# Two gate units moved from between the steps of grouped-query attention into the block-pair stage of a hybrid encoder block

## The chip, the core and the metric

The kernel runs as one program on one core of a Trainium2 chip. The metric is the device time of one execution in microseconds (us), as the median of several runs. Five engines work side by side, each through its own queue of instructions in a fixed order: TensorE (PE, matrix products; its weight loads are listed as PEld), VectorE (DVE), ScalarE (ACT), GpSimd (POOL) and SyncE (SP, which issues most transfers). An instruction starts when those ahead of it on its engine have started or ended and its semaphores are there.

## The reference

One encoder layer over 1024 tokens of width 1024 with three parallel mixers. Cut to what matters here:

```python
h = rms_norm(x, g_pre)
a_qkv, bq, bk, bv, mq, ga, gb, gm, mg = split(h @ w_in)   # one wide projection
oa = dilated window attention of a_qkv (3 groups, softmax-weighted over the groups)
ob = grouped-query attention: 8 query heads, 2 key heads, all 1024 tokens
om = cross-attention into 256 memory rows
ya = (oa * silu(ga)) @ w_br_a
yb = (ob * silu(gb)) @ w_br_b
ym = (om * silu(gm)) @ w_br_m
gates = sigmoid(mg + b_merge)
merged = gates[0] * ya + gates[1] * yb + gates[2] * ym
out = x + rms_norm(merged @ w_out, g_post)
```

The change concerns `ga`, 512 of the columns of `h @ w_in`. They are four *gate units* of 128 columns, named (0, 0) to (0, 3). `gb` is the units (1, 0) to (1, 3), `gm` the units (2, 0) to (2, 3). Each unit ends as g * (1 + tanh(g / 2)), which is twice the silu, and is stored in DRAM (`g2d`).

## The kernel before

Products of h are made in a split form: h and each weight are a high part and a rest (`hh` and `hl`, `wh` and `wl`), and a product of 128 rows by 512 tokens is three matmuls: high by high, high by rest, rest by high.

**A gate unit multiplied plainly** (`add_unit`, L187, and `dense`, L125) loads 512 KB of weights, splits them (ACT L91, DVE L92), and makes for each of two halves of the tokens 8 x 3 = 24 matmuls with a moving tile of 512 columns (PE L129, L131, L133): 48 for a unit, 96 for two. Each half is finished by `evac` in `add_gate` (L198): DVE L200, ACT L201, DVE L202 and a store (L203).

**The attention stage** (`b_att`, L770) is grouped-query attention as 16 groups (8 blocks of 128 queries by 2 key heads), 8 steps to a group. Step n does `row_max` on PE (L781, its minimum taken by DVE L782), and for later stages of earlier steps: `shift` (PE transpose L789, DVE L790), `scores` (PE L799 and L800, exponential on ACT L802, running sum on POOL: L804 for the second key tile of a group, L806 for the third to the eighth), `pv` once in 8 steps (8 matmuls of L815, each listed as two, on plain 32-bit data), and `final` one step behind it: the sum is split (ACT L91 into `blh`, DVE L92 into `bll`) and summed over partitions by two PE matmuls (L111). `q_prep` (four PE transposes L704, ACT L707, DVE L709, ACT L711) comes once in 16 steps.

PE's order is written by hand. `weave` (L162) takes matmuls one at a time from two sources, the queue of gate units and the attention, so that both come to an end together: it compares the share done of each by a table of costs, and so spreads the gate matmuls evenly between the attention's steps. The attention's estimate holds pads (`START_PAD`, `END_PAD`) where it has nothing for PE. Before the change seven units are spread over the attention: (2, 3), (1, 0) to (1, 3), (0, 0) and (0, 1). The other engines' order in this stage comes from a scheduler.

**The pair stage** (from L1326, its products in `pair_product`, L1314) multiplies units two at a time in a Winograd form of Strassen's method: 2 x 2 blocks, seven products in place of eight, each 4 x 3 = 12 matmuls of 512 columns, so 84 for a pair of units. The sums of weight blocks that it needs are POOL's (`k_sum`, L1067), the splits ACT's and DVE's (`k_block`, `k_own`), the sums of results DVE's (`c_add`, `c_fin`). The list `PAIRS` gives the order: 12 pairs of rotary units alternate with the others, which are one pair of gate units, (0, 2) and (0, 3), and 12 pairs of merge units, 25 pairs in all. The weights of pair n are loaded two pairs ahead (`k_load`), in turn into the `wr` buffers and into two tiles named `vA12`. In this stage all engines' orders are written by hand.

Between the two stages lie the products of the values (L1233 and L1284); behind the pairs come the windowed attention, the branch projections and the output.

Of the kernel before, what the change touches and what calls it, by code (L numbers as in the profile page):

```python
# [8 lines left out]
F32 = mybir.dt.float32  # L9
# [8 lines left out]
P = 128  # L18
# [15 lines left out]
def block(ctx: ExitStack, tc: tile.TileContext, x, xT, memT, cst, msk, bcst, tabA, gpost,  # L34
          wu, wv, wb, wmem, wbr, wout, out):
    nc = tc.nc
# [160 lines left out]
    def add_gate(i, p_):  # L197
        def evac(half, p):  # L198
            th = fp["p"].tile([P, 512], F32, name="fth", bufs=2)
            V.tensor_tensor(th, p, rb[:, half * 512:half * 512 + 512], op=OP.mult)  # L200
            A.activation(p, th, AF.Tanh, scale=0.5)  # L201
            V.scalar_tensor_tensor(th, p, 1.0, th, op0=OP.add, op1=OP.mult)  # L202
            nc.sync.dma_start(g2d[i, p_, :, half * 512:half * 512 + 512], th)  # L203
        add_unit(wu[U_G + 4 * i + p_], evac)

    g2d = dram.tile([3, 4, P, S], F32, name="g2d")
# [12 lines left out]
    def pool(name, side="left"):  # L219
        p = tc.tile_pool(name=name, bufs=1, side=side, reuse_waits="tile")  # L220
        return p, p.__enter__()
# [226 lines left out]
    for k in range(8):  # L448
        if k % 2 == 0:
            load_wkv(k // 2)  # L450
        for e in range(2 if k == 0 else 1):
            t = slice(e * 512, e * 512 + 512) if k == 0 else slice(0, S)
# [29 lines left out]
    for c in range(2):  # L482
        t = st.tile([P, 4, 256], F32, name=f"mt{c}", tag=f"xk{c}")
# [209 lines left out]
    half = [slice(0, 512), slice(512, 1024)]  # L693
    with tc.tile_pool(name="ba", bufs=1, reuse_waits="tile") as ba:
# [185 lines left out]
        ng = 0  # L880
        for i in (2, 1, 0):
            for p_ in range(4):
                if (i, p_) not in ((2, 0), (2, 1), (2, 2)) + GATES_P:
                    add_gate(i, p_)
                    ng += 1
        early[len(queue)] = first_values
# [23 lines left out]
    vbp, vb = pool("vb", "right")  # L910
# [128 lines left out]

    TURNS = [(j, c, g) for c in range(2) for g in range(3) for j in (1, 0)]  # L1040
    pairs = [(8 * i + f, 8 * i + f + 1) for i in (2, 1, 0) for f in range(0, 8, 2)]
    others = [("gate", 0)] + [("merge", m) for m in range(12)]
    PAIRS = [x for m in range(12) for x in (("rope", m), others[m])] + [others[12]]
    KR = {}

    def unit_of(n, u):
        kind, m = PAIRS[n]
        if kind == "rope":
            return 2 * m + u
        return U_M + pairs[m][u] if kind == "merge" else U_G + 4 * GATES_P[u][0] + GATES_P[u][1]  # L1050

    def k_load(n, u):

        KR[n, u] = (vb.tile([P, 1024], F32, name=f"vA12{u}") if n % 2 else
                    wp.tile([P, 1024], F32, name="wr", bufs=WR))
        nc.sync.dma_start(KR[n, u], wu[unit_of(n, u)])

# [46 lines left out]
    def kr():  # L1104
        z = next(kr_turn) % 10
        return (vb.tile([P, 512], F32, name=("vy2", "vy3", "vv0", "vv1", "vy0", "vy1")[z]) if z < 6 else
                SPARE[z // 2 - 3][:, half[z % 2]])
# [7 lines left out]
    def c_fin(n, u, t, ps_=None):  # L1115

        r = RV.pop((n, u, t)) if ps_ is None else kr() if n < last else p1
        src = r if ps_ is None else ps_
        kind, m = PAIRS[n]
        if kind != "rope":  # L1120
            V.tensor_tensor(r, src, rb[:, half[t]], op=OP.mult)
            if kind == "gate":
                x = kr()

                def gate_it():
                    A.activation(x, r, AF.Tanh, scale=0.5)
                    V.scalar_tensor_tensor(r, x, 1.0, r, op0=OP.add, op1=OP.mult)
                    nc.sync.dma_start(g2d[GATES_P[u]][:, half[t]], r)
                then.append(gate_it)
            else:  # L1130
                j = pairs[m][u]

                def merge_it():
                    A.activation(r, r, AF.Tanh, scale=0.5, bias=hbm[:, j:j + 1])
                    nc.scalar.dma_start(thd[j, :, half[t]], r)
                then.append(merge_it)
            return
        x = kr()
        if TURNS[m][0]:
            V.tensor_tensor(x, src, tab[0][:, half[t]], op=OP.mult)  # L1140
            V.tensor_tensor(r, src, tab[1][:, half[t]], op=OP.mult)
        else:
            V.scalar_tensor_tensor(x, src, -0.125, tab[0][:, half[t]], op0=OP.mult, op1=OP.mult)
            V.scalar_tensor_tensor(r, src, -0.125, tab[1][:, half[t]], op0=OP.mult, op1=OP.mult)
        RP[m, t, u] = x, r

    def turn_it(n, t):
        kind, m = PAIRS[n]
        if kind != "rope":
            return  # L1150
        g = TURNS[m][2]
        (ac, as_), (bc, bs) = [RP.pop((m, t, z)) for z in range(2)]
        if m not in RO:
            RO[m] = [kp.tile([P, S], F32, name=f"ko{z}") for z in range(2)]
        o1, o2 = RO[m]
        G.tensor_tensor(half_of(o1, t, g), classes(ac, g), classes(bs, g), op=OP.subtract)
        G.tensor_tensor(half_of(o2, t, g), classes(as_, g), classes(bc, g), op=OP.add)

    def k_store(n):
        kind, m = PAIRS[n]  # L1160
        if kind != "rope":
            return
        j, c, g = TURNS[m]
        for u, o in enumerate(RO.pop(m)):
            for h in range(4):
                a = h % 2 * 64 + 32 * u
                nc.sync.dma_start(qkd[j, 2 * c + h // 2, g, a:a + 32], o[h * 32:h * 32 + 32])
# [57 lines left out]
    for n in range(28):  # L1225
        i, k = divmod(n, 4)
# [17 lines left out]
        for stage in (2, 1, 0):  # L1244
            r, at = divmod(n - 6 - (0, 2, 3)[stage], 3)
# [14 lines left out]
        if k == 3:  # L1260
# [4 lines left out]
            7: [lambda: operand(7, 1), lambda: operand(7, 2)], 8: [lambda: v3_split("S3")],  # L1265
            9: [lambda: [nc.sync.dma_start(tab[j], tabA[:, j]) for j in range(2)]],
            13: [lambda: k_load(0, 0), lambda: V.tensor_tensor(tab[1], tab[1], rb, op=OP.mult)],
            17: [lambda: V.tensor_tensor(tab[0], tab[0], rb, op=OP.mult)],
            10: [lambda: v3_sum("S4", "A12", "S2", OP.subtract)], 12: [lambda: v3_split("S4")],
            14: [lambda: v3_sum("S1", "A11", "S2", OP.add)], 16: [lambda: v3_split("S1")],  # L1270
            18: [lambda: k_load(0, 1)], 20: [lambda: v3_split("A22"), lambda: k_load(1, 0)], 22: [lambda: k_load(1, 1)],
            23: [lambda: k_sum(0, 1)], 24: [lambda: k_own(0)], 25: [lambda: [k_sum(0, j) for j in (2, 3)]],
            26: [lambda: k_block(0, "S2")], 27: [lambda: k_block(0, "S1"), lambda: k_block(0, "S3"), lambda: k_sum(0, 4)]}
    for n in range(28):
        i, k = divmod(n, 4)
# [33 lines left out]
    SPARE = [wp.tile([P, 1024], F32, name=x) for x in ("wh", "wl")]  # L1309
    last = len(PAIRS) - 1  # L1310
    BANK = {}
# [90 lines left out]
    for n in range(last + 1):  # L1402
# [31 lines left out]
        if n + 2 <= last:  # L1434
            k_load(n + 2, 0)
# [41 lines left out]
    r = RV[last, 0, 1]  # L1477
# [741 lines left out]
    q, r = ss[7], ss[7][:, 3:4]  # L2219
# [33 lines left out]
ATT_PRIO = 120  # L2253
LA_T, LA_P = 2, 3
FIRST_PAD, LAST_PAD = 7000.0, 2000.0
GATES_P = ((0, 2), (0, 3))
VG = (2, 0, 1)
U_G = 24
U_MQ = 36
U_M = 40  # L2260
# [112 lines left out]
```

## Time and profile before

| What | us |
|---|---|
| median of 3 runs (1364.65 to 1366.45) | 1366.28 |
| the profiled execution, device time | 1364.44 |
| its span, first to last instruction | 1362.5 |
| attention stage, from the first `row_max` on PE to the first matmul of the values | 212.8 to 453.2 |
| pair stage, its 2100 matmuls | 569.86 to 1046.22 |
| PE busy over the span | 1344.7 |

A line of the timeline has the start in us, the duration, the engine, the line of the code, the operation, output and inputs with their shapes, the count that was merged, and in brackets how long the engine was idle ahead of it and what ended that. In a table of windows each engine has its busy time in the stretch and the number of its instructions. Matmuls overlap, so the step from one to the next is read from two starts, not from a duration.

### The profile page before, as it was taken

What the parts mean: (1) busy time and instruction counts of PE and PEld (TensorE: products, weight loads), DVE (VectorE), ACT (ScalarE), POOL (GpSimd) and SP (SyncE); (2) the same over time, 40 slices, a digit from 0 to 9 for tenths busy, and PEclk for the clock granted to TensorE, in tenths of its full rate; (3) what the DMA queues carried; (4) which work ended last, traced back from release to release, by engine and by line L of the source; (5) the groups of instructions that cost most, each with busy time, mean ns of one, the idle gap of its engine ahead of it and who ended that gap; (6) DMA issues with size and microseconds to landing.
All of it is one profiled execution on the core that took longest, in us unless ns stands there. A gap on an engine that the chain in (4) does not pass through costs nothing.

```text
span 1362.5 us, 22863 instructions
## 1 busy us (share of the span) xinstructions
PE 1344.7 (99%) x8303; PEld 1087.4 (80%) x8303; DVE 1016.6 (75%) x1837; ACT 657.1 (48%) x1389; POOL 579.1 (43%) x443
## 2 busy tenths in 40 slices
PE   7999999999999999999999999999999999999997
PEld 7899986666666789988888888888888777778886
DVE  7868677776777498767777776687877666778977
ACT  7544465656655445333343333333335676763332
POOL 0516702676676200244465554555552135662003
PEclk9999999999999999999999999999999999999999
DMA  6346522322244578514333333322347777976445
GB/s 253 109 170 232 179 108 94 104 78 93 74 132 142 210 239 277 164 57 138 99 114 118 108 124 123 115 91 91 107 129 256 233 209 244 279 231 233 146 187 185
DMA packets 125488, 213.80 MB, mean 157 GB/s; under 512 B 32480, under 2 KB 64576, under 8 KB 125376
## 3 DMA queue, kind: packets, MB, share of 16 engines
q1 hardware_dynamic: 116064, 198.42, 44.7%
q10 hardware_dynamic: 9312, 13.93, 2.8%
q8 instruction: 65, 1.06, 0.3%
q14 instruction: 47, 0.39, 0.1%
HBM read 145.92 MB, written 66.38 MB: 156 GB/s over the span
## 4 chain that ended last, share of the span: by engine, by line
PE 93%; DVE 3%; ACT 2%; issue 1%; POOL 1%; DMA 0%; SPq 0%; DVEq 0%; POOLq 0%; ACTq 0%
PE s L1323 35%; PE d L1913 7%; PE s L1233 4%; PE s L2137 4%; PE ov L815 4%; PE sc L2055 3%; PE d L133 3%; PE d L129 3%; PE d L131 3%; PE s L1284 3%; PE s L1597 2%; PE tr L781 2%; PE s L800 2%; PE s L799 2%; PE d L529 2%; PE d L2137 2%
## 5 line engine op out<-in xcount | busy, mean ns | idle before, releaser
L806 POOL TENSOR_TENSOR bl<-bl,bp 128x512 f32<-128x512 f32 x96 | 132.9, 1384 | 52.8 <-ACT bp L802 47.3
L1323 PE MATMUL s<-hh,vS 128*128 128x512 f32 x400 | 131.1, 389 | 0.0
L1323 PE MATMUL s<-vA,vS 128*128 128x512 f32 x450 | 106.1, 389 | 0.0
L92 DVE TENSOR_TENSOR vS<-vot,vS 128x512 fp32r<-128x512 f32 x75 | 89.4, 1193 | 19.9 <-ACT vS L91 19.9
L1323 PEld LDWEIGHTS s<-vA,vS 128*128 128x128 f32 x450 | 84.5, 188 | 17.5
L802 ACT ACTIVATE bp<-s 128x512 f32<-128x512 f32 x128 | 75.7, 595 | 43.2 <-PE s L800 42.2
L782 DVE TENSOR_REDUCE bn<-tr 128x1 f32<-128x512 f32 x128 | 85.2, 683 | 12.5 <-PE tr L781 11.5
L133 PE MATMUL d<-hh,wl 128*128 128x512 f32 x224 | 89.5, 400 | 0.0
L131 PE MATMUL d<-hl,wh 128*128 128x512 f32 x224 | 89.1, 398 | 0.0
L129 PE MATMUL d<-hh,wh 128*128 128x512 f32 x224 | 89.0, 397 | 0.0
L1323 PEld LDWEIGHTS s<-hh,vS 128*128 128x128 f32 x400 | 75.1, 188 | 15.6
L1609 ACT ACTIVATE pra<-pra,sts 128x192 f32<-128x192 f32 (+1 forms) x176 | 72.4, 415 | 13.3 <-DVE sts L1608 13.1
L1323 PE MATMUL s<-hh,wl 128*128 128x512 f32 x200 | 78.1, 390 | 0.0
L1323 PE MATMUL s<-hl,wh 128*128 128x512 f32 x200 | 77.8, 389 | 0.0
L1323 PE MATMUL s<-hh,wh 128*128 128x512 f32 x200 | 77.8, 389 | 0.0
L1323 PE MATMUL s<-hl,vS 128*128 128x512 f32 x200 | 77.8, 389 | 0.0
L1608 DVE CUSTOM_DVE_ANT_0 pra<-s,mask 128x192 f32<-128x192 f32 (+1 forms) x192 | 48.8, 309 | 33.5 <-PE s L1597 20.0
L1327 ACT ACTIVATE vv<-s 128x512 f32<-128x512 f32 x50 | 29.9, 598 | 82.3 <-PE s L1323 48.4
L1067 POOL TENSOR_TENSOR vot<-wr 128x512 f32<-128x512 f32 x13 | 22.2, 1706 | 111.0 <-DVE wl L92 111.0
L815 PE MATMUL ov<-bp,VS 128*64 128x512 f32 x256 | 58.5, 598 | 0.0
L1067 POOL TENSOR_TENSOR vot<-vot,vA 128x512 f32<-128x512 f32 x12 | 19.3, 1606 | 89.7 <-DVE vS L92 89.7
L129 PEld LDWEIGHTS d<-hh,wh 128*128 128x128 f32 x224 | 42.2, 188 | 13.3 <-issue 5.3
(627 smaller groups left out, 4004.6 us busy)
## 6 DMA issues: line engine op xcount, KB each, us to landing
wr<-in_wu SPq DMA_DIRECT2D x40, 512.0 KB
vA<-in_wu SPq DMA_DIRECT2D x24, 512.0 KB
qkd<-ko SPq DMA_DIRECT2D x96, 128.0 KB
wl<-thd SPq DMA_DIRECT2D x24, 512.0 KB
wos<-os SPq DMA_DIRECT2D x12, 512.0 KB
wr<-in_wbr SPq DMA_DIRECT2D x24, 256.0 KB
aq<-qkd SPq DMA_DIRECT2D x12, 512.0 KB
ak<-qkd SPq DMA_DIRECT2D x12, 512.0 KB
```

The costliest lines, as they stand in the source:

```text
L92: V.tensor_tensor(dst_l, src, dst_h.bitcast(F32), op=OP.subtract)
L129: PE.matmul(dst, wh[:, k, :], hh[k][:, t], start=k == 0, stop=False)
L131: PE.matmul(dst, wh[:, k, :], hl[k][:, t], start=False, stop=False)
L133: PE.matmul(dst, wl[:, k, :], hh[k][:, t], start=False, stop=k == 7)
L782: fp["last"] = V.tensor_reduce(st[i]["n"][:, j, c:c + 1], s, axis=AX.X, op=OP.min)
L802: A.activation(pp, s, AF.Exp, scale=-1.0)
L806: G.tensor_tensor(lsum[i % 2], lsum[i % 2], pp, op=OP.add)
L815: PE.matmul(o[e * 64:e * 64 + 64], VS[:, kt, kv], d.pop(kt), start=kt < 2, stop=kt >= NT - 2)
L1323: PE.matmul(BANK[n, c], a, b, start=k == 0 and q == 0 and not more, stop=k == 3 and q == 2, skip_group_check=c in "XW")
L1609: A.activation(src, src, AF.Exp, scale=-1.0, bias=bias, accum_out=sts[:, 1, h, T:T + 1])
L1913: PE.matmul(ps_, a, b, start=k == 0 and q == 0, stop=k == 3 and q == 2)
L2137: PE.matmul(dst[:, e[0]:e[1]], a, b, start=k == 0 and q == 0, stop=k == 3 and q == 2)
```

## The change

The two units (0, 0) and (0, 1) leave the queue of the attention stage, which keeps five. They become a second gate pair, `("gate", 0)`, of the pair stage; the old gate pair becomes `("gate", 1)`. There are 26 pairs: gate pairs stand second and fourth, each merge pair comes one place later among the others, and the list ends in three merge pairs in place of two. So that the last pair still has its weights in `wr`, the turn of the two buffers is counted from the end: the first pair now loads into `vA12`.

```diff
-                if (i, p_) not in ((2, 0), (2, 1), (2, 2)) + GATES_P:
+                if (i, p_) not in ((2, 0), (2, 1), (2, 2)) + sum(GATES_P, ()):
...
-    others = [("gate", 0)] + [("merge", m) for m in range(12)]
-    PAIRS = [x for m in range(12) for x in (("rope", m), others[m])] + [others[12]]
+    others = [("gate", m) for m in range(len(GATES_P))] + [("merge", m) for m in range(12)]
+    PAIRS = [x for m in range(12) for x in (("rope", m), others[m])] + others[12:]
...
-        return U_M + pairs[m][u] if kind == "merge" else U_G + 4 * GATES_P[u][0] + GATES_P[u][1]
+        if kind == "merge":
+            return U_M + pairs[m][u]
+        i, p_ = GATES_P[m][u]
+        return U_G + 4 * i + p_
...
-        KR[n, u] = (vb.tile([P, 1024], F32, name=f"vA12{u}") if n % 2 else
+        KR[n, u] = (vb.tile([P, 1024], F32, name=f"vA12{u}") if (len(PAIRS) - n) % 2 == 0 else
...
-                    nc.sync.dma_start(g2d[GATES_P[u]][:, half[t]], r)
+                    nc.sync.dma_start(g2d[GATES_P[m][u]][:, half[t]], r)
...
-GATES_P = ((0, 2), (0, 3))
+GATES_P = ((0, 0), (0, 1)), ((0, 2), (0, 3))
```

With five units in place of seven `weave` lays the gate matmuls thinner. Three places show it.

The first is PE's order in the middle of the attention, from the `pv` of the eighth group on (L129, L131 and L133 are gate matmuls, L781 a `row_max`, L799 and L800 the scores of one key tile, L111 the two sums of `final`). Before:

```order
L815 MATMUL ov<-bp,VS 64x512 x8
L133 MATMUL d<-hh_88,wl 128x512
L129 MATMUL d<-hh_89,wh 128x512
L131 MATMUL d<-hl_97,wh 128x512
L133 MATMUL d<-hh_89,wl 128x512
L129 MATMUL d<-hh_90,wh 128x512
L131 MATMUL d<-hl_98,wh 128x512
L133 MATMUL d<-hh_90,wl 128x512
L781 MATMUL tr<-KS,QH 128x512
L129 MATMUL d<-hh_91,wh 128x512
L799 MATMUL s_3945<-QH,KS 128x512
L800 MATMUL s_3945<-QL,KB 128x512
```

And of the change:

```order
L815 MATMUL ov<-bp,VS 64x512 x8
L133 MATMUL d<-hh_87,wl 128x512
L129 MATMUL d<-hh_88,wh 128x512
L131 MATMUL d<-hl_96,wh 128x512
L133 MATMUL d<-hh_88,wl 128x512
L129 MATMUL d<-hh_89,wh 128x512
L781 MATMUL tr<-KS,QH 128x512
L799 MATMUL s_3873<-QH,KS 128x512
L800 MATMUL s_3873<-QL,KB 128x512
```

Five gate matmuls follow a `pv` where there were seven, and none stands between the `row_max` and the scores. From one `pv` to the next of the 13 middle periods there are now 13 gate matmuls in each; before there were 17 to 19, 236 in all.

The second is PE's order at the stage's beginning, from the first `q_prep` (L704) on. Before:

```order
L704 MATMUL tr<-cs,qn_1025 128x128 x4
L131 MATMUL d<-hl_93,wh 128x512
L133 MATMUL d<-hh_85,wl 128x512
L129 MATMUL d<-hh_86,wh 128x512
L131 MATMUL d<-hl_94,wh 128x512
L133 MATMUL d<-hh_86,wl 128x512
L129 MATMUL d<-hh_87,wh 128x512
L131 MATMUL d<-hl_95,wh 128x512
L133 MATMUL d<-hh_87,wl 128x512
L129 MATMUL d<-hh_88,wh 128x512
L131 MATMUL d<-hl_96,wh 128x512
L781 MATMUL tr<-KS,QH 128x512
```

And of the change:

```order
L704 MATMUL tr<-cs,qn_1025 128x128 x4
L131 MATMUL d<-hl_93,wh 128x512
L133 MATMUL d<-hh_85,wl 128x512
L129 MATMUL d<-hh_86,wh 128x512
L131 MATMUL d<-hl_94,wh 128x512
L133 MATMUL d<-hh_86,wl 128x512
L129 MATMUL d<-hh_87,wh 128x512
L131 MATMUL d<-hl_95,wh 128x512
L781 MATMUL tr<-KS,QH 128x512
```

Seven gate matmuls lie between `q_prep` and the first `row_max` where there were ten. From there to the first `pv` there are 29 in place of 41. DVE has one L200 and no L202 in that stretch where it had two L200 and one L202.

The third is ACT's order at the stage's end, from the split of the sum of the last group but one (`blh`) on; the L802 behind it is the exponential of the last group's second key tile, L201 belongs to a gate unit, and the next L802 is the third key tile. Before:

```order
L91 ACTIVATE blh<-bl_2700 128x512
L802 ACTIVATE bp<-s_4864 128x512
L817 ACTIVATE obt<-ov 64x512
L201 ACTIVATE d<-fth 128x512
L802 ACTIVATE bp<-s_4898 128x512
```

And of the change:

```order
L91 ACTIVATE blh<-bl_2700 128x512
L802 ACTIVATE bp<-s_4747 128x512
L201 ACTIVATE d<-fth 128x512
L817 ACTIVATE obt<-ov 64x512
L802 ACTIVATE bp<-s_4772 128x512
```

The gate's L201 now stands ahead of L817, and still ahead of the third key tile's exponential. On PE there are 17 gate matmuls between that key tile's scores and the last `final` before the change and 13 behind it. From the `pv` that ends the middle (421.65 us) to the first matmul of the values there are 48 and 34.

## The prediction

> **What bounds the kernel now.** The page's first part comes first: one engine is busy nearly all the time.
>
> ```profile
> PE 1344.7 (99%) x8303; PEld 1087.4 (80%) x8303; DVE 1016.6 (75%) x1837; ACT 657.1 (48%) x1389; POOL 579.1 (43%) x443
> ```
>
> So a matmul fewer is time saved wherever PE stays the engine that others wait for, and the question is what is late next where matmuls go. The chain that ended last, in order of time, gives the two stages:
>
> ```profile
> 234.65 3.58 PE ov L815 x16
> ...
> 421.65 3.58 PE ov L815 x16
> ...
> 569.86 476.36 PE s L1323 x2100
> ```
>
> The last row is the whole pair stage: 2100 matmuls without a break, 476.36 / 2100 = 0.2268 us each. Nothing but PE is on the path there. The other two are the first and the fourteenth `pv`; 13 periods of the attention lie between them, 187.0 / 13 = 14.38 us each. The table of windows cuts the attention into middle, beginning and end:
>
> ```profile
> 234.65:421.65 187.00, 187.00 (x822) 120.73 (x823) 137.39 (x213) 113.55 (x186) 125.94 (x92) 1.00 0.32 104
> 212.80:234.65 21.85, 21.33 (x91) 15.61 (x93) 21.02 (x35) 13.88 (x20) 6.92 (x6) 1.00 0.28 97
> 421.65:453.30 31.65, 31.36 (x135) 18.12 (x135) 16.79 (x21) 16.61 (x30) 20.53 (x16) 1.00 0.20 68
> ```
>
> The columns behind the stretch are its length, then PE, PEld, DVE, ACT and POOL, then clock and DMA. The granted clock is full. In the middle PE has no idle time, DVE 73%, POOL 67%, ACT 61%. In the beginning DVE is busy 21.02 of 21.85 us, as full as PE: here two engines bind together.
>
> **Part 1, what goes.** 96 matmuls leave the attention. Their price is the step between gate matmuls that follow each other:
>
> ```profile
> 425.51 0.40 PE L131 MATMUL d<-hl,wh 128*128 128x512 f32 x1
> 425.75 0.40 PE L133 MATMUL d<-hh,wl 128*128 128x512 f32 x1
> 425.98 0.40 PE L129 MATMUL d<-hh,wh 128*128 128x512 f32 x1
> 426.22 0.40 PE L131 MATMUL d<-hl,wh 128*128 128x512 f32 x1
> 426.45 0.39 PE L133 MATMUL d<-hh,wl 128*128 128x512 f32 x1
> ```
>
> 0.94 us for four steps, 0.235 each: **-22.6 us** if PE stays the bound throughout. At the pair stage's pace it is -21.8, the other end.
>
> **Part 2, what comes.** One pair is 84 matmuls at 0.2268: **+19.05 us**. Its sums, splits and evacuations hide under PE as those of the 25 pairs do: over the pair stage DVE, the fullest helper, is busy 358.81 of 476.36 us.
>
> ```profile
> 569.86:1046.22 476.36, 476.36 (x2101) 393.90 (x2101) 358.81 (x383) 179.12 (x281) 244.37 (x146) 1.00 0.36 118
> ```
>
> A gate pair behind a rotary pair stands at the list's head already, between two rotary pairs and without a break, so the second one meets nothing new. The new turn of buffers puts the first pair into tiles whose last reader, the split of the fifth product of the values, is over before that stage ends; I cost it at nothing. What the loads have as cover is two pairs, 38 us, and without it the pair would wait for 512 KB at a time.
>
> Without any new wait the sum is -22.6 + 19.05 = -3.5 us (-2.7 at one pace for both). The Trainium skill, "TensorE: Matmul & The Clock Gate" (section "Wait — 56ns, not 53.3ns?"), gives one price for a warm matmul of 512 columns, 215.7 ns, wherever it stands. By it the change saves at most 12 x 0.2157 = 2.6 us, an estimate from that page; this trace has two paces, 0.227 and 0.235, both slower, and I go by them.
>
> **Part 3, what is late next.** The 96 matmuls are also cover: 15 of them at the beginning, 67 in the middle, 14 at the end (counted in the order). I take the three apart.
>
> *Beginning.* From `q_prep` to the first `row_max` runs a fixed chain through ACT:
>
> ```profile
> 209.71 0.60 PE L704 MATMUL tr<-cs,qn 128*128 128x128 f32 x4
> ...
> 212.79 0.50 PE L781 MATMUL tr<-KS,QH 128*128 128x512 f32 x1 [0.16 <-ACT QH L711]
> ...
> 220.28 0.50 PE L781 MATMUL tr<-KS,QH 128*128 128x512 f32 x1 [0.34 <-DVE bn L782]
> ```
>
> The chain is 3.08 us and PE waited for its end already, so the three matmuls that go there (0.7 us) save nothing. Behind it `row_max` waits for DVE to free a bank (third row). 12 matmuls go, 2.8 us; DVE loses one L200 and one L202, at 0.69 and 0.68:
>
> ```profile
> L202 DVE SCALAR_TENSOR_TENSOR fth<-d,fth 128x512 f32<-128x512 f32 x10 | 6.8, 683 | 0.7 <-ACT d L201 0.7
> L200 DVE TENSOR_TENSOR fth<-d,rb 128x512 f32<-128x512 f32 x9 | 6.2, 686 | 2.3 <-PE d L133 2.2
> ```
>
> Were DVE the bound all along, 1.4 of the 2.8 us would be lost; in the stretch's second half DVE has short waits for PE, so I take 0.5. Lost at the beginning: 0.7 + 0.5 = **1.2** (ends: 0 and the whole 3.5).
>
> *Middle.* 67 matmuls in 13 periods are 5.15 each, 1.21 us, so the period falls to 14.38 - 1.21 = 13.17. DVE had 137.39 / 13 = 10.6 us of work in it, POOL 9.7, ACT 8.7, and gate work goes from DVE and ACT; none reaches 13.17. What can bind is a loop. POOL's is the tightest: the sum's last addition, ACT's `blh`, the next group's exponential, L804, six L806.
>
> ```profile
> 266.46 1.31 POOL L804 TENSOR_TENSOR bl<-bp 128x512 f32<-128x512 f32 x1 [1.22 <-ACT bp L802]
> 270.63 8.92 POOL L806 TENSOR_TENSOR bl<-bl,bp 128x512 f32<-128x512 f32 x6 [2.87 <-ACT bp L802]
> 282.49 1.29 POOL L804 TENSOR_TENSOR bl<-bp 128x512 f32<-128x512 f32 x1 [2.94 <-ACT bp L802]
> ```
>
> Without the 2.87 us of waiting for PE's third key tile the loop is 8.92 + 2.94 + 1.29 = 13.15 us where ACT's four copies of `q_prep` stand in it (last row), and 1.22 + 1.31 + 8.92 = 11.45 where they don't (first row). They take turns, so the mean is 12.3 against 13.17: it fits, by 0.9 us. The other tight place is the shift: its DVE step L790 must end before the new group's scores, which the order puts 7 matmuls (1.6 us) behind the transpose in every second period, 7 to 9 before. Ahead of L790 DVE has a minimum of 0.68 and, in token periods, a subtraction:
>
> ```profile
> L782 DVE TENSOR_REDUCE bn<-tr 128x1 f32<-128x512 f32 x105 | 70.3, 683 | 11.9 <-PE tr L781 11.1
> L790 DVE TENSOR_TENSOR QL<-tr,cs 4x512 fp32r<-4x512 f32 x13 | 9.0, 689 | 0.4
> L742 DVE TENSOR_TENSOR tb<-tx,tb 128x512 f32<-128x512 f32 x8 | 6.9, 858 | 0.1
> ```
>
> 0.68 + 0.69 fits into 1.6, with 0.86 more it is 2.2, up to some 0.5 us short. Lost in the middle: 0 at one end, 13 x 0.5 = 6.5 at the other; since it takes the subtraction, a full queue and the short order together, I take two such waits, **1.0**.
>
> *End.* With no `row_max` left the last groups run through POOL:
>
> ```profile
> 440.98 0.60 ACT L201 ACTIVATE d<-fth 128x512 f32<-128x512 f32 x1 [1.35 <-DVE fth L200]
> ...
> 442.35 8.06 POOL L806 TENSOR_TENSOR bl<-bl,bp 128x512 f32<-128x512 f32 x6 [1.93 <-ACT bp L802]
> ...
> 450.44 0.63 ACT L91 ACTIVATE blh<-bl 128x512 fp32r<-128x512 f32 x1 [4.18 <-POOL bl L806]
> 451.11 0.69 DVE L92 TENSOR_TENSOR bll<-bl,blh 128x512 fp32r<-128x512 f32 x1 [8.79 <-ACT blh L91]
> ...
> 451.85 0.40 PE L111 MATMUL tr<-bll,one 128*1 128x512 f32 x1 [0.16 <-DVE bll L92]
> ```
>
> PE's last sum waited for this chain already, by 0.16 us. The chain starts with the third key tile's exponential, which still stands behind the gate's L201. Four matmuls go between that tile's scores and the last sum, 0.94 us, and all of it becomes waiting; the reordered L817 adds part of its 0.6. Lost at the end: **1.2** (ends: 0 and 14 x 0.235 = 3.3).
>
> **Sum.** -22.6 + 19.05 + 1.2 + 1.0 + 1.2 = -0.1 us. The profiled execution took 1364.44 (span 1362.5 and 1.9 around it), 1.84 below the median of the runs, 1366.28, and within their spread but for 0.2. Against the median the forecast is **1366.2 us**. A measurement of this kernel tells about 0.2% from no change, 2.7 us: below 1363.5 is faster, above 1369.0 slower.
>
> **The rivals.**
>
> *The cover holds.* Losses of half a microsecond in all, and -3.0 us: 1363.3. For it: no row of PE waiting for another engine in the middle window, and every helper under 80%. Against: PE's waits at the beginning and the end stand in the rows above, where 29 of the 96 matmuls go. To be faster by over 0.2% the three losses may sum to 0.8 at most; 0.7 is gone in the first row of the beginning. Chance 0.13.
>
> *The middle turns from PE to a loop* (slower). Mechanism: the `row_max` minimum, the subtraction and L790 on DVE, and POOL's sum, come later than PE in each period. Price: 0.5 us x 13 = 6.5, with 1.2 and 1.2 outside: 1366.28 - 3.5 + 8.9 = 1371.7. It decides from 13 waits of 0.3 us on. For it: POOL's loop with `q_prep` is as long as the new period. Against: it is that long only every second time. POOL's additions also differ much with what runs beside them:
>
> ```profile
> L806 POOL TENSOR_TENSOR bl<-bl,bp x96: 1266/1287/2126, 228.7 to 449.1; 128x512 f32<-128x512 f32 x96
> ```
>
> At 1.6 in place of 1.49 each (8.92 / 6) the mean loop would be 13.0. The Trainium skill, "SBUF — State Buffer" (section "Who interferes with whom"), has a cause: a VectorE operation with two SBUF inputs and a GpSimd operation that reads SBUF shut each other out. By that rule a shorter period, with the same DVE operations in it, blocks additions more often; the spread of 1266 to 2126 ns agrees. Chance 0.14.
>
> *The 26th pair doesn't run at PE's pace*, because a buffer turns too early or a load stands behind a store on SP; 20% of a pair, 3.8 us, gives 1370. For it: a rotary or gate pair takes eight of the ten result tiles that go round, a merge pair four, and now five such pairs stand in a row at the list's head, three before. Against: 2100 matmuls without a gap. Chance 0.03.
>
> *The forecast*, within 0.2%: 0.70. So faster 0.13, same 0.70, slower 0.17. The range leaves out the tails of the faster and slower cases: from 1362.8, where nothing is lost, to 1370.2, with 4 us lost beyond the forecast; all losses at their far ends together would reach 1376 and are left out.
>
> **What would show it.** The pair stage: 2184 matmuls in 495.4 us; a longer one makes part 2 wrong. The first to the fourteenth `pv`: 13 x 13.17 = 171.3 us by part 1, 172.3 with my losses; above 175 the slower rival is true, and the waits of PE then name L790 or L782 on DVE or ACT's exponentials. From `q_prep` to the first `pv`: 24.9 before, 22.6 forecast. From the fourteenth `pv` to the first matmul of the values: 31.6 before, 29.5 forecast. Anything that moves the time behind the pairs, whose code is the same, would be outside this account.

## The result, and the profile after

| What | before | after |
|---|---|---|
| median of the runs, us | 1366.26 | 1377.37 (1375.86 to 1377.52) |
| ratio, with its 95% interval | | 1.0081 (1.0064 to 1.0099) |
| span of the profiled execution | 1362.5 | 1375.7 |
| q_prep to the first matmul of the values | 243.5 | 236.7 |
| the matmuls of the pairs | 476.4 | 495.6 |

The change costs 11 us. The forecast was 1366.2, in a range that ended at 1370.2. The table of windows, at the forecast's three cuts, says where the time is (length, then PE, PEld, DVE, ACT, POOL, then clock, DMA and GB/s). After the change:

```profile
210.65:234.01 23.36, 21.82 (x91) 14.44 (x91) 22.14 (x38) 15.96 (x24) 6.86 (x6) 1.00 0.24 86
234.01:417.12 183.11, 176.42 (x755) 109.69 (x756) 137.18 (x209) 111.73 (x185) 125.62 (x93) 0.98 0.30 95
417.12:447.36 30.24, 28.75 (x121) 14.96 (x120) 14.31 (x17) 14.40 (x26) 19.78 (x15) 1.00 0.23 76
```

The middle takes 183.11 us where 172.3 was forecast: 10.8 of the 11.2 us of the miss. PE, which had no idle time there, now has 6.7 us of it, and the clock column reads 0.98 in place of 1.00. The pair stage, in the chain of waits, is as forecast:

```profile
564.20 495.55 PE s L1326 x2184
```

The table of PE's waits from the first `row_max` to the values names what PE waits for (total us, times, longest):

```profile
PE tr L781 <- DVE bn L782: 5.9, 4, 2.5
PE s L799 <- ACT bp L802: 1.6, 2, 0.9
PE tr L781 <- ACT QH L711: 0.9, 1, 0.9
```

The longest one is followed back through three timelines of the changed kernel. PE first:

```profile
308.33 0.40 PE L800 MATMUL s<-QL,KB 68*128 68x512 f32 x1
311.20 0.77 PE L781 MATMUL tr<-KS,QH 128*128 128x512 f32 x1 [2.47 <-DVE bn L782]
311.76 0.63 PE L131 MATMUL d<-hl,wh 128*128 128x512 f32 x1
312.19 0.63 PE L799 MATMUL s<-QH,KS 128*128 128x512 f32 x1
312.62 0.63 PE L800 MATMUL s<-QL,KB 68*128 68x512 f32 x1
```

A `row_max` has no free bank until the minimum of an earlier one is taken. On DVE that minimum is queued behind L818, which waits for ACT's copy of the attention's output:

```profile
309.77 0.68 DVE L818 TENSOR_TENSOR obt<-obt,ov 64x512 f32<-64x512 f32 x1 [0.49 <-ACT obt L817]
310.38 1.27 DVE L782 TENSOR_REDUCE bn<-tr 128x1 f32<-128x512 f32 x2
```

And on ACT that copy (L817) stands last in a queue whose head waits 4.14 us for GpSimd:

```profile
303.79 0.63 ACT L91 ACTIVATE blh<-bl 128x512 fp32r<-128x512 f32 x1 [4.14 <-POOL bl L806]
304.33 0.57 ACT L707 ACTIVATE QH<-tr 64x512 fp32r<-64x512 f32 x1
304.81 0.58 ACT L802 ACTIVATE bp<-s 128x512 f32<-128x512 f32 x1
305.41 0.60 ACT L707 ACTIVATE QH<-tr 64x512 fp32r<-64x512 f32 x1
306.03 0.60 ACT L802 ACTIVATE bp<-s 128x512 f32<-128x512 f32 x1
306.66 1.29 ACT L711 ACTIVATE QH<-QH 64x512 fp32r<-64x512 f32 x2
307.97 1.15 ACT L736 ACTIVATE tx<-tx,cs 128x1024 f32<-128x1024 f32 x1
309.15 0.59 ACT L817 ACTIVATE obt<-ov 64x512 f32<-64x512 f32 x1
```

Each of the eight instructions ahead of it (L711 is two) is short, but the copy comes late by all of them. L736 scales a block of tokens that VectorE reads at 327.7 us at the earliest. GpSimd itself is not late here: its sum ends 1.3 us ahead of the end of the `pv`, in the middle's other groups 1.0 to 2.8 us. What differs is how much stands between the split and the copy. The same run of instructions stands around 339 us, with a wait of 2.07. And the wait is not the whole price. Before it a step is 0.23 us; in PE's rows behind it each step is 0.43. The windows (same columns) show the granted clock:

```profile
308.00:310.00 2.00, 0.73 (x4) 0.24 (x2) 1.51 (x3) 1.95 (x3) 0.00 (x1) 1.00 0.36 135
310.00:312.00 2.00, 0.80 (x2) 0.74 (x3) 1.65 (x3) 1.31 (x3) 1.41 (x2) 0.75 0.78 246
312.00:314.00 2.00, 2.00 (x6) 1.54 (x6) 1.05 (x3) 0.60 (x1) 1.12 (x1) 0.50 0.26 67
```

So the two places cost more than their waits. The periods that hold them were 17.1 and 16.8 us; the undisturbed ones take 13.6 and 13.0 in turn, and these two stand in places of 13.0, so they cost 4.1 and 3.9. Of the rest most is in the last period, 15.3 us: waits of 0.86 and 0.60 us at 410 and 413 us, where the copy stands behind a gate's L201 and VectorE's addition behind a gate's splits and L202.

The first theory follows from this. **Theory 1**: two accidents of ScalarE's order, which the scheduler makes from its own estimate of PE's pace, cost about 8 of the 11 us; take the scalings out of the way and they are back. **Theory 2**: with 13 gate matmuls in a period in place of 18 there is no slack left, and whatever the order, a wait removed comes back elsewhere. **Theory 3**: the clock falls by itself where the filling is thin.

### The profile page after: what moved, and what is told of

Its sections match the earlier page's. It is cut to its first block, busy times and chain, and to the rows that moved or that the text cites. A ratio compares the mean times of both kernels' runs of the same rounds, so it can differ in the third digit from the quotient of the medians.

```text
span 1375.7 us, 22865 instructions
## 1 busy us (share of the span) xinstructions
PE 1349.2 (98%) x8291; PEld 1086.4 (79%) x8291; DVE 1026.2 (75%) x1844; ACT 660.2 (48%) x1396; POOL 588.7 (43%) x447
## 4 chain that ended last, share of the span: by engine, by line
PE 89%; DVE 5%; ACT 2%; POOL 1%; issue 1%; DMA 1%; SPq 0%; DVEq 0%; ACTq 0%; POOLq 0%
PE s L1326 36%; PE d L1916 7%; PE s L1236 4%; PE s L2140 4%; PE sc L2058 3%; PE ov L815 3%; PE s L1287 3%; PE s L1600 2%; PE d L131 2%; PE d L133 2%; PE d L129 2%; PE tr L781 2%; PE s L799 2%; PE s L800 2%; PE d L529 2%; PE d L2140 2%
## 5 line engine op out<-in xcount | busy, mean ns | idle before, releaser
L1326 PE MATMUL s<-hh,vS 128*128 128x512 f32 x416 | 136.4, 389 | 0.0
L1326 PE MATMUL s<-vA,vS 128*128 128x512 f32 x468 | 110.3, 389 | 0.0
L1326 PEld LDWEIGHTS s<-vA,vS 128*128 128x128 f32 x468 | 87.9, 188 | 18.2
L782 DVE TENSOR_REDUCE bn<-tr 128x1 f32<-128x512 f32 x128 | 85.1, 684 | 15.0 <-PE tr L781 14.0
L802 ACT ACTIVATE bp<-s 128x512 f32<-128x512 f32 x128 | 75.7, 595 | 38.3 <-PE s L800 36.5
L131 PE MATMUL d<-hl,wh 128*128 128x512 f32 x192 | 77.1, 401 | 0.0
L133 PE MATMUL d<-hh,wl 128*128 128x512 f32 x192 | 76.9, 400 | 0.0
L129 PE MATMUL d<-hh,wh 128*128 128x512 f32 x192 | 76.6, 399 | 0.0
L1070 POOL TENSOR_TENSOR vot<-vA 128x512 f32<-128x512 f32 x13 | 23.3, 1795 | 106.6 <-ACT wh L91 106.6
L92 DVE TENSOR_TENSOR wl<-wr,wh 128x1024 fp32r<-128x1024 f32 x29 | 35.5, 1224 | 41.3 <-ACT wh L91 41.2
L1070 POOL TENSOR_TENSOR vot<-vot,wr 128x512 f32<-128x512 f32 x13 | 20.9, 1606 | 95.0 <-DVE vS L92 95.0
L781 PE MATMUL tr<-KS,QH 128*128 128x512 f32 x128 | 52.7, 412 | 6.9 <-DVE bn L782 5.9
```

The costliest lines, as they stand in the source:

```text
L92: V.tensor_tensor(dst_l, src, dst_h.bitcast(F32), op=OP.subtract)
L129: PE.matmul(dst, wh[:, k, :], hh[k][:, t], start=k == 0, stop=False)
L131: PE.matmul(dst, wh[:, k, :], hl[k][:, t], start=False, stop=False)
L133: PE.matmul(dst, wl[:, k, :], hh[k][:, t], start=False, stop=k == 7)
L781: PE.matmul(s, QH[:, kv * 4 + j], KS[:, kv, c * 512:c * 512 + 512], start=True, stop=True)
L782: fp["last"] = V.tensor_reduce(st[i]["n"][:, j, c:c + 1], s, axis=AX.X, op=OP.min)
```

## The experiments

Ratios are to the kernel before as measured beside each run, so they compare better than the medians. "Middle" is from the first to the fourteenth `pv` in the run's own profile; without any wait it is 171.3 us by the forecast, and 187.0 before. The summary first:

| run | kernel and edit | ratio to before (95%) | middle, us |
|---|---|---|---|
| after | the change as it is | 1.0081 (1.0064 to 1.0099) | 183.1 |
| e1 | scalings behind the copy | 1.0072 (1.0060 to 1.0085) | 178.8 |
| e2 | scalings at their use | 1.0048 (1.0034 to 1.0062) | 177.3 |
| e11 | split of the sums behind the copy | 1.0065 (1.0052 to 1.0077) | 178.5 |
| e5 | e1 and e11 | 1.0049 (1.0036 to 1.0061) | 174.8 |
| e6 | e5, `final` one step later | 1.0031 (1.0019 to 1.0042) | 174.2 |
| e7 | e2 and e11, `final` one step later | 1.0025 (1.0015 to 1.0035) | 174.7 |
| e10 | e7, `final` two steps later | 1.0003 (0.9994 to 1.0012) | 171.5 |
| e12 | e10, more filling at the beginning | 1.0004 (0.9995 to 1.0013) | 171.3 |
| e8 | the change, a sixth unit in the attention | 1.0083 (1.0067 to 1.0098) | 180.8 |
| e3 | before, with e5's edits | 0.9999 (0.9991 to 1.0008) | 187.1 |
| e13 | before, with e10's edits | 1.0021 (1.0012 to 1.0029) | 190.1 |

### The scalings behind the copy (e1)

```diff
-                A.activation(t, t, AF.Copy, scale=cs[:, ...])
+                with tc.issue_after(fp["obt" if k else "copy"].ins): A.activation(t, t, AF.Copy, scale=cs[:, ...])
...
-                A.activation(d["ob"], o[64:128], AF.Copy)
+                fp["obt"] = A.activation(d["ob"], o[64:128], AF.Copy)
```

> The changed kernel, with ScalarE's eight scalings of the token blocks (L736, 1.15 us each) kept behind the copy of the attention's output (L817) that is issued last; nothing else is edited. Theory 1 (two accidents of ScalarE's order): the two long waits of TensorE at 311.2 and 341.5 us in the changed kernel (2.47 and 2.07 us) came because L736 stood ahead of L817, so VectorE's add (L818) and the minima behind it (L782) came late; with their slow-clock stretches they cost 4.2 + 3.9 us. Expected: 1377.4 - 8 = 1369 us (1368 to 1371), first to fourteenth values block 175 us in place of 183.1, and a granted clock of 1.00 in every 2 us of it. Theory 2 (thinner filling: whatever the order, the waits come back elsewhere): 1375 to 1378 us, 183 us. Theory 3 (the clock dips by itself when the filling is thin): the waits go, the dips stay: 1373 to 1375 us.

Measured: 1374.61 us (the kernel before, beside it, 1364.97), so theory 1's 8 us are not there: the ratio's interval overlaps that of the change. In the profiled executions the middle is 4.3 us shorter, about half of the 8. The mechanism was read rightly as far as it goes. ACT's copy now stands one place earlier, the wait is shorter by 0.98 us, most of one scaling (1.15), and no slow stretch follows it. PE in this run:

```profile
310.34 0.48 PE L781 MATMUL tr<-KS,QH 128*128 128x512 f32 x1 [1.49 <-DVE bn L782]
310.65 0.40 PE L131 MATMUL d<-hl,wh 128*128 128x512 f32 x1
```

The clock is 1.00 in every 2 us of the stretch, so theory 3 falls. But 1.49 us of the 2.47 stay: the rest of the queue (the head that waits for GpSimd, four copies of QH) is as late as it was. The waits of the last period stay as well, 0.82 and 0.61 us.

### The scalings at their use (e2)

In place of the tie the eight scalings are issued later in the program, behind the latest exponential, at the step before the subtraction that reads them.

```diff
+                scale[24 * k + 24 + 2 * j] = (t, cs[:, ...])
...
+                    if n in scale:
+                        with tc.issue_after(fp["exp"].ins): A.activation(scale[n][0], scale[n][0], AF.Copy, scale=scale[n][1])
```

> The changed kernel, with the same eight scalings issued later in the program (two and four steps ahead of the subtractions that read them, behind the latest exponential), so that none stands near the copy of the output. Theory 1: the same as in the run before, 1369 us (1368 to 1371), since it matters only that they leave the place ahead of L817. Theory 2: 1375 to 1378 us. If instead a scaling ahead of the exponentials is as bad as one ahead of the copy, waits of TensorE for bp (L802) take the place of those for bn: 1371 to 1375 us.

Measured: 1371.71 us, between the two theories. A wait of 1.46 us for bn stands at 311 us as before, now with no scaling near it. The copy starts at 308.38, and the seven instructions ahead of it are the split, which waited 4.12 us for GpSimd, the four copies of QH and two exponentials: it is the head of the queue that makes the wait.

### Split of the row sums behind the copy (e11), and both (e5)

```diff
-                split(lh, ll, lsum[i % 2])
+                with tc.issue_after(fp["obt"].ins): A.activation(lh, lsum[i % 2], AF.Copy)
+                V.tensor_tensor(ll, lsum[i % 2], lh.bitcast(F32), op=OP.subtract)
```

> The other half of the pair of ties alone: the changed kernel with the split of the row sums (blh) behind the copy of the output; the scalings stand where the scheduler puts them, at the two troubled places still right ahead of the copy. With the first run and the run with both ties it tells which of the two is the root. If it is the scaling ahead of the copy: the waits at the two places stay at 1.2 us or more, and the time at 1.006 to 1.008 times before (the changed kernel is at 1.008). If it is the wait of ScalarE's head for GpSimd, behind which the copies, the scaling and the output then queue up: ScalarE does the scaling in that time, the waits for bn go, and the time is that of both ties, 1.004 to 1.006 times before.

> The changed kernel with both ties: the scalings and the split of the row sums (blh, which waits up to 4.14 us for GpSimd) behind the copy of the output, so that ScalarE's order is the same in every block. Theory 1: at least the 8 us of the first run, and up to 2 more if the small waits (0.4 to 0.9 us each) go too: 1366 to 1369 us. Theory 2: 1375 to 1378 us. If the late copy was only one of several bounds (VectorE's minima next), 1370 to 1373 us.

Measured: 1.0065 alone, 1.0049 with both. Alone it takes the waits for bn out of the middle but for 0.2 us, as the second theory of its expectation has it: the root is ScalarE's head that waits for GpSimd. But the time is not that of both ties, because the scaling still stands ahead of the copy and so of the split (near 305 us it waits 1.39 us for its own load), and PE meets the split's end instead. PE's waits in the run with the split alone:

```profile
PE tr L111 <- DVE bll L820: 5.1, 8, 1.0
PE tr L111 <- ACT blh L819: 1.3, 1, 1.3
```

and with both ties:

```profile
PE tr L111 <- DVE bll L820: 2.1, 5, 0.5
PE tr L111 <- ACT blh L819: 1.3, 1, 1.3
```

This is theory 2 in part: the wait has moved from L781 to L111, the sum over partitions in `final`, which was one step behind `pv` and had no wait longer than 0.33 us in the changed kernel. It is smaller there, so both ties gain, but it is the same time coming back.

### `final` later (e6, e7, e10), and more filling ahead (e12)

```diff
-LAG_S, LAG_T, LAG_P, LAG_F = 10, 12, 14, 15
+LAG_S, LAG_T, LAG_P, LAG_F = 10, 12, 14, 16
```

> The run with both ties, with the last piece of a block (the sum over partitions of blh and bll, L111, and what leaves with it) one step later: LAG_F 16 in place of 15. In the run with both ties no wait for bn was left; TensorE waited at L111 for bll and blh instead (0.48, 0.53, 0.44, 1.28 + 0.40 and 0.21 us, and a granted clock of 0.56 to 0.59 for 4 us behind the 1.28). Theory 1 (each wait that TensorE meets is one of ScalarE's or VectorE's order, and costs its own length and a slow stretch if it is long): these go, 1371.5 - 4 to 5 = 1366 to 1368 us, ratio to before 1.001 to 1.002. Theory 2 (POOL's sums, 13.15 us for a block of 13.2, bound the stage, so the wait moves with the reader): 1370 to 1372 us, ratio 1.004 to 1.005, with waits for POOL's bl behind blh.

> The changed kernel with the scalings issued later (as in the second run), the split of the row sums behind the copy of the output, and LAG_F 16. Theory 1: as the run beside it, less what the scalings ahead of the exponentials still cost there: ratio 1.000 to 1.002 to before, first to fourteenth values block 172.3 to 174 us (171.3 is the forecast without any wait). Theory 2: ratio 1.004 to 1.005.

Measured: 1.0031 and 1.0025, between the theories again. In e7 the first ten periods are regular, 12.9 to 13.5 us, as the forecast had them; then one is 15.89. There PE waits 1.50 us at L111 for a split that took 1.71 us where the others take 0.68 (e6 has the same). DVE and POOL at that moment:

```profile
372.61 1.71 DVE L820 TENSOR_TENSOR bll<-bl,blh 128x512 fp32r<-128x512 f32 x1
```

```profile
372.51 2.96 POOL L806 TENSOR_TENSOR bl<-bl,bp 128x512 f32<-128x512 f32 x2 [3.03 <-ACT bp L802]
```

GpSimd's addition, the first of the two in the row, started 0.10 us earlier and ended 0.55 us ahead of the subtraction's end, and the subtraction with two inputs in SBUF took 1.03 us longer than usual. The Trainium skill, "SBUF — State Buffer" (section "Who interferes with whom"), has the rule that such a pair shuts each other out and that the one issued first decides; this row agrees.

The next step is LAG_F 17:

> The run with the scalings issued later, the split behind the copy and LAG_F 16, with LAG_F 17. In the run with 16, fourteen blocks kept 12.9 and 13.5 us in turn but for one of 15.89 us, where TensorE waited 1.50 us at L111 for a bll that took 1.71 us in place of 0.68. If that is the last wait in the middle: 2.4 us less, 1.0000 to 1.0015 times before, first to fourteenth values block 172.3 us. If it comes back as another wait (minima, QL): as the run with 16, 1.0025.

Measured: 1.0003, and the middle that part 1 gave without any wait, 171.3 us, to a quarter of a microsecond (with 168 gate matmuls in it, one fewer than in the change). Its windows:

```profile
209.80:233.42 23.62, 21.88 (x91) 14.39 (x91) 22.19 (x38) 13.95 (x23) 6.40 (x5) 1.00 0.25 85
233.42:404.96 171.54, 171.54 (x753) 107.50 (x755) 133.98 (x209) 110.86 (x188) 126.80 (x93) 1.00 0.32 101
404.96:434.69 29.73, 28.42 (x121) 15.45 (x122) 14.00 (x17) 14.33 (x26) 21.49 (x16) 1.00 0.26 83
```

PE has no idle time in the middle, with the same five units between the steps. So theory 2 falls as far as it says that thin filling must wait: neither GpSimd's sums nor VectorE's minima bind at 13.2 us a period. It holds in that each single repair gave only a part. From `q_prep` to the values e10 takes 224.9 us, 18.6 less than before, and the pairs take 19.1 more: that is why the time is the old one. LAG_F 17 without the other two edits was not run.

> The same, with 22 in place of 16 filling steps ahead of the first row minimum (six more steps of 300 in the plan, so about two to three gate matmuls move from the blocks to the beginning). The first minimum waited 0.86 us there for ScalarE's copies of QH, 0.16 in the kernel before. If the beginning's losses are waits of that fixed chain: 0.5 to 0.7 us less than the run beside it. If the blocks are then too thin for GpSimd's sums (13.15 us a block): 1 to 3 us more.

Measured: 1.0004 beside 1.0003. The first minimum's wait fell from 0.86 to 0.40 us, as expected, and the stretch from `q_prep` to the values from 224.9 to 224.4 us in the profiled executions. The device time can't tell half a microsecond: its interval is 1.2 us to either side. The 1 to 3 us more for thinner blocks did not come; the middle is 171.3 us.

### A sixth unit (e8)

```diff
+        add_gate(0, 0, g2x)
+        ng += 1
         early[len(queue)] = first_values
```

> Dose: the changed kernel with one of the two moved gate units multiplied in the attention as well (twice in all; its second copy goes to a spare array), so 6 units fill the blocks in place of 5 or 7. ScalarE's order is left to the scheduler, and the scalings stand ahead of the copy of the output in it here too. 48 matmuls of 0.235 us add 11.3 us. If the filling hides such orders (theory 1 with filling as cover): with three matmuls more in a block most of the 8 us of long waits go, so the changed kernel + 11.3 - 6 to 9 = 1.002 to 1.004 times the changed kernel, 1.010 to 1.012 times before. If the waits are there whatever the filling: 1.008 times the changed kernel, 1.016 times before.

Measured: 1.0083, beside 1.0081 for the change, so 48 matmuls more cost nothing that can be told, and neither expectation held: the one for cover gave the sixth unit too little. From `q_prep` to the values it is 243.5 us with seven units, 234.7 with six, 236.7 with five. The seventh unit's going saved 8.8 of its 11.3 us; the sixth's going cost 2.0. With six units PE's waits in the whole attention are short:

```profile
PE tr L782 <- ACT QH L712: 0.6, 1, 0.6
PE tr L782 <- DVE bn L783: 0.4, 1, 0.4
```

though scalings stand right ahead of the copy there too (at 251.68 and 293.46 us, for instance). So the loss begins between six units and five. How much of that is cover and how much is order e8 doesn't tell, for its orders are its own: VectorE's addition is never more than 2.9 us late in it, and up to 4.8 in the change.

### The same edits in the kernel before (e3, e13)

> Control: the kernel before the change, with the scalings behind the copy of the output and the split of the row sums (blh) behind it too. Theory 1: with 18 filling matmuls per block nothing of ScalarE's order reaches TensorE, so 1366.3 us within 1. If the ties help by themselves, whatever the filling: below 1365 us.

> Control for the best version: the kernel before with the same three edits (scalings at their use, split of the row sums behind the copy, LAG_F 17). With them the changed kernel came to 1.0003 times before (0.9994 to 1.0012). If the edits only undo what the thinner filling laid open, they do nothing where the filling is thick: 0.999 to 1.001, and the change itself is then worth about nothing once the orders are right. If they are worth something by themselves: below 0.998, and the change still costs the difference.

Measured: 0.9999 with the ties, so they are worth nothing by themselves. With all three edits it is 1.0021, slower, which the expectation did not have. Its middle is 190.1 us; beside one wait of 1.21 us ahead of it for a gate half (L202) the trace shows nine steps 0.15 to 0.49 us too long, eight of them ahead of a `row_max` or a `q_prep`, together 2.3 of the 3.1 us that this middle is longer than the old one. Why the later `final` makes them was not tried. So the edits of e10 fit the thin filling only; under the same edits the change is worth 1.0003 against 1.0021, and against the kernel before as it was it is worth nothing.

### The clock by itself (e9)

```diff
+                if x == 2 and i in (4, 6, 8, 10, 12):
+                    with tc.issue_after(fp["last"].ins):
+                        V.tensor_reduce(dmy, KS[:, 0, None, 0:512].bitcast(F32).to_broadcast([P, i, 512]), axis=AX.XY, op=OP.min)
```

> Probe of the clock in the kernel before: in five blocks (i = 4, 6, 8, 10, 12) VectorE has one more reduction, of i times 512 elements, right behind the third row minimum; by the 0.68 us of a minimum of 512 these take 2.5 to 8 us, and with the filling as it is TensorE waits the part of it that its free banks don't cover: about nothing in the first to 4 or 5 us in the last. If a wait of over 2 us alone lowers the granted clock (as behind the waits of 2.47 and 2.07 us in the changed kernel, not behind those of 1.49 and less), each wait of over 2 us is followed by 3 to 4 us at 0.43 us a matmul, and none of under 1.5 us is. If the dips belong to the thin filling: none here.

One execution was measured. The five reductions took 2.29 to 6.55 us. Behind the first three, up to 4.42 us, no step of PE is more than 0.2 us late: so much the kernel before covers. Behind the fourth and fifth it waits 2.41 and 2.17 us, and each time the clock goes down. PE at the first of these:

```profile
358.13 0.40 PE L111 MATMUL tr<-blh,one 128*1 128x512 f32 x1
360.94 0.40 PE L111 MATMUL tr<-bll,one 128*1 128x512 f32 x1 [2.41 <-DVE bll L92]
...
361.97 0.63 PE L804 MATMUL s<-QH,KS 128*128 128x512 f32 x1
362.39 0.63 PE L805 MATMUL s<-QL,KB 68*128 68x512 f32 x1
```

The two periods are 18.9 and 18.6 us, 4.0 more than the same periods before, for waits of 2.41 and 2.17: the slow steps cost another 1.6 to 1.8 us. So it doesn't take thin filling, and theory 3 falls here too: a wait of 2.1 to 2.5 us costs about 4, as the two in the changed kernel did (4.1 and 3.9).

## Why the prediction was wrong

**Part 1, the price of the 96 matmuls**: right. In e10, with no wait left in the middle, it is 171.54 us where part 1 gave 171.3.

**Part 2, the pair**: right, 495.55 against 495.4 us, and none of the rivals about buffers or loads showed.

**Part 3, beginning and end**: nearly right. From `q_prep` to the first `pv` 23.4 us, 22.6 forecast; from the fourteenth `pv` to the values 30.2, 29.5 forecast. Together 1.5 us beyond the 2.4 counted. The first minimum does wait for ACT's copies, 0.86 us, as the fixed chain said.

**Part 3, the middle**: the step that failed. It says of the helpers' work "none reaches 13.17. What can bind is a loop.", looks at the two tightest loops, and takes 1.0 us, from ends of 0 and 6.5. Measured: 11.8 beyond part 1, so that the time, 1377.4, lies even above the 1376 that the prediction had for all its losses at their far ends. Neither loop did it: in e10 both run in the same 13.2 us and PE waits for neither. What the step left out is that an engine's queue is in order. It compared busy time with the period, and the loops' lengths with it, but not how late an instruction can come because of what happens to stand ahead of it: ACT was busy 113.55 of 187 us before, and yet its copy of the output started, after the change, at 309.15, 4.2 us behind the end of the `pv` that it copies (that one starts at 301.41, and a `pv` takes 3.58 us). Before the change such an order existed without harm, a gate's L201 and this scaling ahead of a copy that starts 2.3 us behind the end of its `pv`, as late as any in that middle:

```profile
296.69 1.14 ACT L736 ACTIVATE tx<-tx,cs 128x1024 f32<-128x1024 f32 x1
297.86 0.59 ACT L817 ACTIVATE obt<-ov 64x512 f32<-64x512 f32 x1
298.48 0.68 DVE L818 TENSOR_TENSOR obt<-obt,ov 64x512 f32<-64x512 f32 x1 [1.00 <-ACT obt L817]
```

with no wait of PE behind it. The prediction read this absence of waits as room, though it shows only that the room was enough for 18 matmuls a period.

How much is covered can be read from the same rows. VectorE's addition (L818) starts behind the end of its `pv` by 4.78, 4.38 and 3.29 us at the three places of the changed kernel, by 3.83, 3.18 and 3.26 in e1, and by 3.80 and 3.27 in e2. PE then waits for `bn` 2.47, 2.07 and 0.86 us, 1.49, 0.85 and 0.82, and 1.46 and 0.84: each time 2.3 to 2.4 us less. So with 13 gate matmuls in a period 2.3 to 2.4 us of lateness are covered. In the kernel before the addition is at most 2.9 us late, and PE doesn't wait. The third `row_max` behind a `pv` is due 4.28 us behind its end there (295.54 to 299.82 us). In the changed kernel it is due at 3.59: the `pv` ends at 405.35, and the matmul ahead of it starts at 408.71, so that without a wait it would start a step of 0.23 later. By an estimate from these rows the old filling covers about 0.7 us more, 3.0. By this estimate the thinner cover is the smaller part of the two long waits; the larger part is that the copy, and with it the addition, comes later than anywhere before the change. The old kernel with the new order was not run. The probe, which holds VectorE up later in the period, has its border between 4.4 us, which were covered, and 5.5, which were not.

The second thing left out is the clock. A wait was priced at its length; behind two of them PE ran at half its pace for about 3.4 us, which cost another 1.7 and 1.8 us.

**The rivals.** The slower one gave a sign to look for, a middle above 175 us; that came true, and PE's waits do name L782 and the exponentials, as it said; the price it named, 1371.7, was 5.7 short. Its mechanism was another: half a microsecond in each of 13 periods from loops, where the runs show two long waits and some short ones from the orders on ScalarE and VectorE. That e1, which should have removed those two, gave back only about half of them shows that the first reading after the result was too simple as well. What the runs establish: the whole loss hangs on orders in the chain copy, split, minimum and last sum, three places (scaling, split, the step of `final`). Each of the three edits that were run alone (e1, e2, e11) gave back less than half of the 0.81% by its ratio; scaling, split and `final` together gave back all but the losses at beginning and end. The later `final` was run only on top of the others. That the scheduler built those orders from an estimate of PE's pace was argued and not tried.

## What to carry to other kernels

When filling work is taken out of a stage, look not at how busy the helpers are but at how late each of their instructions can start behind what stands ahead of it in its queue, above all behind a head that waits for a third engine; no wait in the trace before says only that the old filling was enough. Measure how much: hold one engine up on purpose, a little longer each time, until the bound engine waits. And price a wait of over 2 us of TensorE at 1.7 to 1.9 times its length, as the four here cost.

## What the hardware showed beside

The granted clock falls after waits well under 3 us: behind 2.47, 2.41, 2.17 and 2.07 us the steps of a 512-column matmul went from 0.23 to 0.43 us for about 3.4 us, and behind 1.50, 1.49, 1.47 and 1.46 they didn't. The border isn't sharp in the length of a wait: in e5 two waits close together, 1.28 and 0.40 us, were followed by a slow stretch, and in e11 the same two, at 430.92 and 431.71 us, were not.

Each trace also records when the granted clock changes. In the changed kernel it is first full at 10.64 us, half at 311.01, full at 314.42, half at 341.73 and full at 345.14. These are 300.37, 3.41, 27.31 and 3.41 us apart, which is 88, 1, 8 and 1 steps of 3.413 us. In e5 the first fall comes 419.84 us behind the first full clock, 123 steps, and in e9 348.16 us, 102 steps. So the clock changes only at the ends of equal steps, which the waits don't move. The first full clock comes at 10.39 to 13.08 us in the fourteen traces, so the steps fall differently in each execution. The windows cut at these steps, in the changed kernel:

```profile
307.60:311.01 3.41, 1.13 (x5) 0.56 (x4) 2.92 (x5) 3.33 (x6) 0.91 (x2) 1.00 0.43 137
311.01:314.42 3.41, 3.22 (x8) 2.60 (x9) 2.10 (x5) 0.90 (x2) 2.43 (x3) 0.50 0.44 135
```

In e5:

```profile
426.83:430.24 3.41, 1.73 (x8) 1.10 (x8) 1.90 (x3) 2.60 (x6) 1.29 (x1) 1.00 0.38 132
430.24:433.65 3.41, 3.41 (x10) 2.63 (x9) 0.00 (x0) 1.68 (x3) 2.63 (x3) 0.50 0.12 26
```

And in e11:

```profile
427.24:430.66 3.42, 2.39 (x10) 1.43 (x8) 2.72 (x4) 1.51 (x3) 2.28 (x2) 1.00 0.41 153
430.66:434.07 3.41, 2.75 (x12) 1.89 (x12) 1.00 (x2) 2.52 (x5) 1.78 (x2) 1.00 0.34 106
434.07:437.48 3.41, 3.41 (x16) 1.61 (x16) 0.00 (x0) 1.86 (x4) 3.25 (x3) 1.00 0.05 10
```

In e5 both waits lie in one step, and PE is idle for 1.68 of its 3.41 us; in e11 the end of a step, at 430.66 us, parts them into 1.03 and 0.66. Counted like this over all steps of the fourteen traces from the first full clock on, every step with 1.92 us or more of idle PE is followed by the half clock, and none with 1.47 us or less. Between them 1.68 us was, and 1.55, 1.63 and 1.81, all at a program's end, were not. So about half of a step idle is enough by these traces, and whether a wait of 1.5 to 2 us costs more than its length depends on where it falls.

The Trainium skill, "TensorE: Matmul & The Clock Gate" (section "What's actually happening"), has the clock halved after an idle window of about 3.4 us that runs freely, whatever the kernel does. The steps of 3.413 us, which run freely, and the halved pace agree with it; that 1.7 to 2.4 us of idle time in a step suffice does not agree with an idle time of a whole window.
